# Products with v of even and odd heads in turn, in the two halves of TensorE's columns

## The chip, the cores and the metric

The kernel runs on one core of a Trainium2 chip. The metric is the time of one execution on the device in microseconds (us), the median of three runs.

The engines are TensorE (PE, matrix products and transposes), VectorE (DVE), ScalarE (ACT), GpSimd (POOL) and SyncE (SP, which issues most DMAs). Operands lie in SBUF, products land in banks of PSUM.

## The reference, cut to what matters

Two blocks are computed on 256 rows of 1024 channels in fp32: a feed-forward part, a mixer, a second feed-forward part, then an attention with forget gates ("fox") and a sparse attention ("dsa"). The change touches the mixer alone. It projects its input to q, k, v (8 heads of 64 channels) and u, runs an attention with a bias by relative position over q, k and v, a pooling over u, and projects both through `w_out`:

```python
def one_chunk(c):
    qb = lax.dynamic_index_in_dim(qc, c, axis=1, keepdims=False)
    kb = lax.dynamic_slice_in_dim(kp, c * CHUNK, BAND, axis=1)
    vb = lax.dynamic_slice_in_dim(vp, c * CHUNK, BAND, axis=1)
    s = jnp.einsum('bqhd,bkhd->bhqk', qb, kb).astype(jnp.float32) * scale + bias
    ...
    p = jax.nn.softmax(s, axis=-1)
    return jnp.einsum('bhqk,bkhd->bqhd', p.astype(vb.dtype), vb)

def hybrid_mixer(h, w_in, ..., w_out):
    ...
    a = chunked_attention(q, k, v, q_gain, k_gain, rel_bias)
    p = multiscale_pool(u, pool_w, pool_scale)
    return jnp.concatenate([a, p], axis=-1) @ w_out
```

## The kernel before

The 256 rows are two tiles, t = 0 and 1, of 128. Weights arrive as units of up to 128 x 1024 numbers (tile `raw`); ACT rounds each to fp32r (`whi`, L196), DVE takes the rest (`wlo`, L197), and a product with weights is three one-pass products into an `mm` bank (`half`, with `mm` at L163). `prefetch` keeps up to eight split units ahead. All products of the program are recorded at L163 and all transposes at L178; so the tiles' names tell them apart: `mm` with `op` is the projection of the pooling, `mm` with `oa` that of the attention, `sc` with `kT, qT` (or their parts) the scores, `tr` with `cst, s` the transposes of the softmax, `sc` with `pT, v` the products with v.

The order of the source around the change is made by a planner. `self.now` is a clock that each product and each transpose moves on by a fixed amount (0.109 us for a transpose). `later(us, fn)` puts a step on a heap with a due time, `when(keys, us, fn)` does so once events have fired, and `pump`, called behind every `half`, runs all steps that are due; `drain` runs all. The due times are in `DUE`: `mix_pv` 1.0, `mix_pv2` 4.74. The compiler then orders each engine's instructions by itself: they do not all run in the order of the source.

In the mixer, `scores(t, b)` multiplies q by k for a block of heads: t = 0 has one block of eight heads with 128 keys, t = 1 has two blocks of four heads with 256 keys. Even heads (e = 0) lie in channels 0 to 63 of each 128, odd heads (e = 1) in 64 to 127, and the two take turns, each in a `sc` bank of its own. Then, for each e, DVE adds the bias (L534), ACT and DVE compute the softmax (L443, L445, L538, L540), and `pv(t, b, e)` is planned. It transposes the probabilities in four products into a `tr` bank (`p_T`; there are two such banks) and copies them to a tile `pT` (L466; in turn by ACT and DVE; two buffers). Then `pv2(t, b, e)` runs four fp32 products with v, 64 columns of the array by 128 numbers, into partitions 64 e to 64 e + 63 of a `sc` bank `aT[t]`. Behind the last of a tile, `split_psum` (L238, L239) makes the fp32r pair `oa`, which the projection reads.

The output projection is issued around it: first the four halves on the pooling's result for t = 0, four for t = 1, then, behind a `drain`, the eight on the attention's. So there are projection products that do not need the attention while its steps wait for ACT and DVE.

Of the kernel before, what the change touches and what calls it, by code (L numbers as in the profile page):

```python
# [9 lines left out]
F32 = mybir.dt.float32  # L10
# [6 lines left out]
P = 128  # L17
# [28 lines left out]
def unit_list():  # L46
# [38 lines left out]
DUE = {  # L85
    "ffn_T": 6.0,
    "ffn_x": 3.0,
    "mix_T": 9.32,
    "mix_pool1": 1.21,
    "mix_pool2": 1.49,  # L90
    "mix_s": (0.5, 0.55, 3.0),
    "mix_pv": 1.0,
    "mix_pv2": 4.74,
# [20 lines left out]
class Kern:  # L114
# [330 lines left out]
            nc.scalar.activation(s[:, h, :], s[:, h, :], AF.Exp, bias=m[:, h:h + 1],  # L445
                                 accum_out=l[:, col + h:col + h + 1])

    def p_T(self, pool, s, nh, nk, split=False):

        ps = self.bank("tr")  # L450
        if split:
            n = nk // P
            v = ps.rearrange("p (k h q) -> p k h q", k=n, q=P)
            for k in range(n):
                for h in range(nh):
                    self.tr(v[:, k, h, :], s[:, h, k * P:(k + 1) * P])
            out = tuple(pool.tile([P, n, nh * P], F32R, name="pT" + c, bufs=2) for c in "hl")
            self.split_psum(*(o.rearrange("p k n -> p (k n)") for o in out), ps)
            return out
        v = ps.rearrange("p (h k q) -> p h k q", h=nh, q=P)  # L460
        for h in range(nh):
            for k in range(nk // P):
                self.tr(v[:, h, k, :], s[:, h, k * P:(k + 1) * P])
        out = pool.tile([P, 512], F32, name="pT", bufs=2)
        self.flip = not getattr(self, "flip", False)
        (self.nc.scalar.copy if self.flip else self.nc.vector.tensor_copy)(out, ps)  # L466
        return out.rearrange("p (h k q) -> p h k q", h=nh, q=P)


    def mixer(self, u, gain, next_gain):  # L470
        self.stage = "mix"
        nc, tc, A = self.nc, self.tc, self.A
        with tc.tile_pool(name="mix", bufs=1, reuse_waits="tile") as pool:
# [14 lines left out]
            v = [pool.tile([P, 512], F32, name=f"v{t}") for t in range(2)]  # L488
# [31 lines left out]
            def scores(t, b):  # L520

                nh, nk = (4, P) if t == 0 else (2, S)
                ps = [self.bank("sc").rearrange("p (h k) -> p h k", h=nh) for _ in range(2)]
                for i in range(nh):
                    for e in range(2):
                        j, r = nh * b + i, slice(64 * e, 64 * e + 64)
                        if t == 0:
                            self.mm(ps[e][:, i, :], qT[r, j, :], kT[r, j, :], True, True)
                        else:
                            self.mm3(ps[e][:, i, :], qTs, kTs, True, True, (r, j), (r, j))  # L530
                for e in range(2):
                    s = pool.tile([P, nh, nk], F32, name="s", bufs=6)
                    h0 = 2 * nh * b + e
                    nc.vector.tensor_tensor(s, ps[e], B[:, h0:h0 + 2 * nh - 1:2, S - nk:S], op=ALU.add)  # L534
                    l = self.small("ml", 4, bufs=4)
                    self.softmax_part(pool, s, nh, nk, l, 0)
                    ri = self.small("ri", 4, bufs=4)
                    nc.vector.reciprocal(ri[:, :nh], l[:, :nh])  # L538
                    for i in range(nh):
                        nc.vector.tensor_scalar(s[:, i, :], s[:, i, :], ri[:, i:i + 1], None, op0=ALU.mult)  # L540
                    self.when([("mix", "v")], DUE["mix_pv"], lambda e=e, s=s: pv(t, b, e, s, nh, nk))

            aT = {}

            def pv(t, b, e, s, nh, nk):
                pT = self.p_T(pool, s, nh, nk)
                self.later(DUE["mix_pv2"], lambda: pv2(t, b, e, pT, nh, nk))

            def pv2(t, b, e, pT, nh, nk):
                if b == e == 0:  # L550
                    aT[t] = self.bank("sc").rearrange("p (i q) -> p i q", i=4)
                for i in range(nh):
                    j = nh * b + i
                    for k in range(nk // P):
                        self.mm(aT[t][64 * e:64 * e + 64, j, :], v[k][:, 128 * j + 64 * e:128 * j + 64 * e + 64],
                                pT[:, i, k, :], k == 0, k == nk // P - 1)
                if e == 1 and nh * (b + 1) == 4:
                    self.split_psum(*oT[t, "a"], aT[t])

            dT = {}  # L560
# [28 lines left out]
            for t, acc in self.chunk(u, 4):  # L589
                qk_norm(acc, t, qT, qTs if t else None, _GAIN["q"], 0.125)  # L590
            u += 4
            self.when([("mix", "T", g, t) for g in (_GAIN["k"], _GAIN["q"]) for t in range(1)], DUE["mix_s"][0],
                      lambda: scores(0, 0))
            for b in range(2):
                self.when([("mix", "T", g, t) for g in (_GAIN["k"], _GAIN["q"]) for t in range(2)],
                          DUE["mix_s"][1 + b], lambda b=b: scores(1, b))
# [622 lines left out]
```

## Time and profile before

| | us |
|---|---|
| median of 3 runs | 729.85 (729.18 to 730.84) |
| the profiled execution | 731.11 |
| its span, from the first to the last instruction | 729.3 |
| PE busy in the span | 713.9 |
| DVE busy | 493.7 |
| ACT busy | 366.6 |

The profile shows one execution. PE is TensorE with its products, PEld its weight loads, which overlap with products. An fp32 product appears as two records, a transpose or an fp32r product as one. Products are pipelined and their ends are modelled, so starts are more exact than ends; merged rows give the start of the first and the time to the end of the last. The granted clock (PEclk) is a share of full speed.

### The profile page before, as it was taken

To read this page: it belongs to the slowest core of one execution; us is meant where nothing else is said; L and a number is where in the kernel's file an instruction comes from. 1 tells how busy PE (TensorE), PEld (TensorE's weight loads), DVE (VectorE), ACT (ScalarE), POOL (GpSimd) and SP (SyncE) were. 2 spreads that over 40 slices of the span, in tenths; PEclk is the share of its full clock that TensorE was granted. 3 is DMA by queue.
4 is the path that set the end of the run, shared out by engine and by line. 5 is a ranking of instruction groups with operands and counts; after the bars stand their busy time and mean duration, and the time that the engine had idled before them with its cause. 6 is when DMAs were issued, how large, how long until landed. Compare 5 with 4: busy or idle time off the path is not lost.

```text
span 729.3 us, 9860 instructions
## 1 busy us (share of the span) xinstructions
PE 713.9 (98%) x3608; PEld 597.6 (82%) x3608; DVE 493.7 (68%) x791; ACT 366.6 (50%) x544; POOL 58.2 (8%) x89
## 2 busy tenths in 40 slices
PE   8999999999999999999999999999999999999995
PEld 7788889888888778888889878878987889778984
DVE  6876766665647958665676556663555868998965
ACT  5654554354555736454454354554554625675820
POOL 0011110200003001101111200000000001000001
PEclk9999999999999999999999999999999999999998
DMA  7898656876735245667755767653560427533501
GB/s 261 296 320 294 228 205 217 272 266 195 264 103 204 85 149 171 209 202 252 264 200 198 275 217 229 237 158 111 193 232 29 143 66 253 208 116 116 173 1 58
DMA packets 42034, 139.80 MB, mean 192 GB/s; under 512 B 5362, under 2 KB 6530, under 8 KB 41858
## 3 DMA queue, kind: packets, MB, share of 16 engines
q1 hardware_dynamic: 37890, 127.23, 51.7%
q0 software_dynamic: 3808, 11.56, 4.6%
q8 instruction: 28, 0.46, 0.2%
q10 hardware_dynamic: 288, 0.39, 0.1%
q14 instruction: 20, 0.16, 0.1%
HBM read 132.34 MB, written 6.82 MB: 191 GB/s over the span
## 4 chain that ended last, share of the span: by engine, by line
PE 73%; DMA 11%; DVE 9%; issue 2%; ACT 2%; POOL 2%; SPq 0%; DVEq 0%; POOLq 0%; ACTq 0%
PE mm L163 63%; PE sc L163 6%; DVE wlo L197 4%; DMA raw<-in_w 3%; PE tr L178 3%; DMA hd<-d 3%; DMA d<-hb 2%; DMA rope<-in_rope 1%; POOL hrs L291 1%; ACT whi L196 1%; DMA row_final_norm<-in_final_norm 1%; PE tr L163 1%; POOL d L281 1%; DMA x<-in_x 1%; ACT s L445 0%
## 5 line engine op out<-in xcount | busy, mean ns | idle before, releaser
L197 DVE TENSOR_TENSOR wlo<-raw,whi 128x1024 fp32r<-128x1024 f32 (+3 forms) x236 | 273.9, 1175 | 86.4 <-ACT whi L196 82.8
L196 ACT CAST whi<-raw 128x1024 fp32r<-128x1024 f32 (+3 forms) x236 | 235.5, 1013 | 133.0 <-PE mm L163 82.5
L163 PE MATMUL mm<-whi,xl 128*128 128x512 f32 (+3 forms) x760 | 287.9, 380 | 1.6 <-DVE xl L325 0.8
L163 PE MATMUL mm<-wlo,xh 128*128 128x512 f32 (+3 forms) x760 | 284.1, 374 | 0.5 <-DVE wlo L197 0.2
L163 PE MATMUL mm<-whi,xh 128*128 128x512 f32 (+3 forms) x760 | 283.4, 374 | 0.0
L163 PEld LDWEIGHTS mm<-whi,xl 128*128 128x128 f32 x760 | 143.6, 189 | 25.8 <-DVE xl L325 1.0
L163 PEld LDWEIGHTS mm<-whi,xh 128*128 128x128 f32 x760 | 143.4, 189 | 24.0
L163 PEld LDWEIGHTS mm<-wlo,xh 128*128 128x128 f32 x760 | 143.7, 189 | 23.6 <-DVE wlo L197 1.8
L163 PE MATMUL mm<-whi,hl 128*128 128x512 f32 x176 | 68.7, 390 | 0.0
L163 PE MATMUL mm<-wlo,hh 128*128 128x512 f32 x176 | 68.5, 389 | 0.0
L163 PE MATMUL mm<-whi,hh 128*128 128x512 f32 x176 | 68.5, 389 | 0.0
L239 DVE TENSOR_TENSOR hl<-hd,hh 128x512 fp32r<-128x512 f32 (+1 forms) x24 | 14.5, 644 | 62.4 <-ACT hh L238 62.4
L238 ACT CAST hh<-hd 128x512 fp32r<-128x512 f32 (+1 forms) x24 | 12.8, 582 | 70.8 <-DMA hd<-d 70.8
L163 PEld LDWEIGHTS mm<-whi,hh 128*128 128x128 f32 x176 | 33.0, 188 | 6.9
L163 PEld LDWEIGHTS mm<-whi,hl 128*128 128x128 f32 x176 | 33.0, 188 | 6.8
L163 PEld LDWEIGHTS mm<-wlo,hh 128*128 128x128 f32 x176 | 33.1, 188 | 6.7
L281 POOL DMA_DIRECT2D d<-hb x48 | 26.4, 556 | 148.2 <-DVE hb L413 148.0
L400 ACT ACTIVATE th<-mm,hr 128x512 f32<-128x512 f32 (+1 forms) x24 | 15.6, 651 | 24.8 <-PE mm L163 24.8
L445 ACT ACTIVATE s<-s,nmax 128x128 f32<-128x128 f32 (+1 forms) x48 | 21.3, 446 | 12.8 <-DVE nmax L443 12.7
L291 POOL TENSOR_TENSOR rs<-ms,mhalf 128x1 f32<-128x1 f32 x10 | 6.5, 647 | 181.8 <-DVE ms L304 181.8
L402 DVE SCALAR_TENSOR_TENSOR a<-th,mm 128x512 f32<-128x512 f32 (+1 forms) x24 | 15.1, 630 | 5.2 <-ACT th L400 5.2
L411 DVE SCALAR_TENSOR_TENSOR h<-a,qr,mm 128x512 f32<-128x512 f32 (+1 forms) x24 | 16.7, 698 | 2.3 <-PE mm L163 2.3
(223 smaller groups left out, 598.6 us busy)
## 6 DMA issues: line engine op xcount, KB each, us to landing
raw<-in_w SPq DMA_DIRECT2D x208, 512.0 KB, 4.5
d<-hb POOLq DMA_DIRECT2D x40, 128.0 KB, 4.3
hd<-d POOLq DMA_DIRECT2D x10, 512.0 KB, 6.2
raw<-in_w SPq DMA_DIRECT2D x12, 344.0 KB, 3.2
raw<-in_w SPq DMA_DIRECT2D x8, 372.0 KB, 3.7
raw<-in_w SPq DMA_DIRECT2D x8, 256.0 KB, 4.6
x<-in_x SPq DMA_DIRECT2D x2, 512.0 KB, 4.6
B<-in_bias SPq DMA_DIRECT2D x1, 1024.0 KB, 5.6
```

The costliest lines, as they stand in the source:

```text
L163: self.nc.tensor.matmul(out, a, b, start=start, stop=stop)
L178: self.nc.tensor.transpose(out, a, self.ident[:p, :p])
L196: nc.scalar.copy(hi[:, :m], raw[:, :m])
L197: nc.vector.tensor_sub(lo[:, :m], raw[:, :m], hi[:, :m].bitcast(F32))
L238: nc.scalar.copy(hi, src)
L239: nc.vector.tensor_sub(lo, src, hi.bitcast(F32))
L281: self.nc.gpsimd.dma_start(out=d[a].rearrange("b i m -> i b m"), in_=src[32 * a:32 * a + 32])
L291: self.nc.gpsimd.tensor_tensor(out, a, self.mhalf[:, 0:1].to_broadcast(list(a.shape)), op=ALU.pow)
L400: nc.scalar.activation(th[:, :w], acc[:, :w], AF.Tanh, scale=hr[t])
L402: nc.vector.scalar_tensor_tensor(a[t][:, :w], th[:, :w], 1.0, acc[:, :w], op0=ALU.add, op1=ALU.mult)
L411: nc.vector.scalar_tensor_tensor(h[:, :w], a[t][:, :w], qr[t], acc[:, :w], op0=ALU.mult, op1=ALU.mult)
L445: nc.scalar.activation(s[:, h, :], s[:, h, :], AF.Exp, bias=m[:, h:h + 1], accum_out=l[:, col + h:col + h + 1])
```

## The change

`pv` and `pv2` of a block now handle both parities. `scores` collects the two tiles `s` in a list and plans one `pv` behind the loop instead of one per parity; `pv` transposes and copies both and plans one `pv2`, which issues eight products with e as the innermost loop, so that neighbours in the source write the two halves of the partitions of `aT[t]`. The tile `pT` of the mixer has four buffers instead of two. The number of products, transposes and copies is the same.

```diff
-    def p_T(self, pool, s, nh, nk, split=False):
+    def p_T(self, pool, s, nh, nk, split=False, bufs=2):
...
-        out = pool.tile([P, 512], F32, name="pT", bufs=2)
+        out = pool.tile([P, 512], F32, name="pT", bufs=bufs)
...
+                ss = []
                 for e in range(2):
                     s = pool.tile([P, nh, nk], F32, name="s", bufs=6)
+                    ss.append(s)
...
-                    self.when([("mix", "v")], DUE["mix_pv"], lambda e=e, s=s: pv(t, b, e, s, nh, nk))
+                self.when([("mix", "v")], DUE["mix_pv"], lambda: pv(t, b, ss, nh, nk))
 
             aT = {}
 
-            def pv(t, b, e, s, nh, nk):
-                pT = self.p_T(pool, s, nh, nk)
-                self.later(DUE["mix_pv2"], lambda: pv2(t, b, e, pT, nh, nk))
-
-            def pv2(t, b, e, pT, nh, nk):
-                if b == e == 0:
+            def pv(t, b, ss, nh, nk):
+                pT = [self.p_T(pool, s, nh, nk, bufs=4) for s in ss]
+                self.later(DUE["mix_pv2"], lambda: pv2(t, b, pT, nh, nk))
+
+            def pv2(t, b, pT, nh, nk):
+
+                if b == 0:
                     aT[t] = self.bank("sc").rearrange("p (i q) -> p i q", i=4)
                 for i in range(nh):
                     j = nh * b + i
                     for k in range(nk // P):
-                        self.mm(aT[t][64 * e:64 * e + 64, j, :], v[k][:, 128 * j + 64 * e:128 * j + 64 * e + 64],
-                                pT[:, i, k, :], k == 0, k == nk // P - 1)
-                if e == 1 and nh * (b + 1) == 4:
+                        for e in range(2):
+                            self.mm(aT[t][64 * e:64 * e + 64, j, :], v[k][:, 128 * j + 64 * e:128 * j + 64 * e + 64],
+                                    pT[e][:, i, k, :], k == 0, k == nk // P - 1)
+                if nh * (b + 1) == 4:
                     self.split_psum(*oT[t, "a"], aT[t])
```

## Rows read from the trace of the kernel before

**Rows 1.** The page's first part: busy us (share of the span) and instructions.

```profile
PE 713.9 (98%) x3608; PEld 597.6 (82%) x3608; DVE 493.7 (68%) x791; ACT 366.6 (50%) x544; POOL 58.2 (8%) x89
```

**Rows 2.** Chain of waits in order of time, 246 to 275: start, us, what.

```profile
247.30 1.58 PE sc L163 x11
...
262.64 10.90 PE mm L163 x47
```

**Rows 3.** Windows of 5 us: busy us (instructions) by engine, granted clock, DMA share, GB/s.

```profile
250.00:255.00 5.00, 5.00 (x31) 3.79 (x31) 5.00 (x14) 3.21 (x12) 0.00 (x0) 1.00 0.00 0
255.00:260.00 5.00, 5.00 (x31) 3.13 (x29) 1.85 (x5) 1.17 (x2) 0.00 (x0) 1.00 0.33 108
```

**Rows 4.** PE in order of time, products with v: start us, us, what, count.

```profile
251.89 0.40 PE L163 MATMUL mm<-whi,op 128*128 128x512 f32 x1
252.21 1.09 PE L163 MATMUL sc<-pT,v 128*64 128x128 f32 x8
253.23 0.50 PE L163 MATMUL mm<-whi,op 128*128 128x512 f32 x1
253.57 0.40 PE L163 MATMUL mm<-wlo,op 128*128 128x512 f32 x1
...
256.24 0.65 PE L163 MATMUL sc<-pT,v 128*64 128x128 f32 x4
256.82 0.66 PE L178 MATMUL tr<-cst,s 128*128 128x128 f32 x4
...
262.57 0.50 PE L163 MATMUL mm<-wlo,op 128*128 128x512 f32 x1
```

**Rows 5.** PE grouped by line and form, 252.3 to 262.5: busy us, mean ns, idle before.

```profile
L163 PE MATMUL sc<-pT,v 128*64 128x128 f32 x48 | 6.7, 282 | 0.0
L163 PE MATMUL mm<-whi,op 128*128 128x512 f32 x5 | 2.4, 478 | 0.0
L178 PE MATMUL tr<-cst,s 128*128 128x128 f32 x12 | 2.1, 286 | 0.0
L163 PE MATMUL mm<-wlo,op 128*128 128x512 f32 x2 | 0.8, 397 | 0.0
```

**Rows 6.** PE in order of time, the scores of tile 0, row halves in turn.

```profile
236.28 1.16 PE L163 MATMUL sc<-kT,qT 64*128 64x128 f32 x16
237.37 0.50 PE L163 MATMUL mm<-whi,xl 128*128 128x512 f32 x1
```

**Rows 7.** Weight loads and products, 260.05 to 260.2, where an odd block meets an even one.

```profile
260.10 0.20 PEld L163 LDWEIGHTS sc<-pT,v 128*64 128x64 f32 x4 [0.17 <-issue]
260.11 0.33 PE L163 MATMUL sc<-pT,v 128*64 128x128 f32 x2
```

**Rows 8.** PE in order of time, scores of tile 1: first block's ends, second block's ends.

```profile
245.14 0.39 PE L163 MATMUL sc<-kTsh,qTsl 64*128 64x256 f32 x2
...
245.84 0.29 PE L163 MATMUL sc<-kTsh,qTsh 64*128 64x256 f32 x2
...
247.30 0.38 PE L163 MATMUL sc<-kTsh,qTsl 64*128 64x256 f32 x1 [0.26 <-DVE s L534]
...
248.60 0.28 PE L163 MATMUL sc<-kTsh,qTsh 64*128 64x256 f32 x1
```

**Rows 9.** DVE in order of time: weight split, scalings, the copies that waited [idle before].

```profile
253.24 1.20 DVE L197 TENSOR_TENSOR wlo<-raw,whi 128x1024 fp32r<-128x1024 f32 x1
254.36 0.61 DVE L540 TENSOR_SCALAR s<-s,ri 128x256 f32<-128x256 f32 x2
...
255.69 0.69 DVE L466 COPY pT<-tr 128x512 f32<-128x512 f32 x1 [0.65 <-PE sc L163]
...
260.58 0.69 DVE L466 COPY pT<-tr 128x512 f32<-128x512 f32 x1 [3.07 <-PE sc L163]
```

**Rows 10.** Tile pT, 245 to 264, who waited for it: us, times.

```profile
PEld sc L163: 0.2, 1
```

**Rows 11.** PE in order of time, the first projection product on the attention.

```profile
267.92 0.39 PE L163 MATMUL mm<-whi,oa 128*128 128x512 f32 x1
```

**Rows 12.** PE's waits behind 252 us: us in total, times, longest (first of seven).

```profile
PE tr L178 <- DVE y L915: 1.0, 1, 1.0
```

## The prediction, made before the result was seen

> **What bounds the kernel now.** I read the page first. TensorE (PE) is busy for 98% of the span, its weight loads, which run under the products, for 82%, and the next engine, VectorE (DVE), for 68% [rows 1], so time that leaves PE's queue should leave the span unless something else is waiting right behind it. Next, the chain of waits over the mixer's attention. From 247.30 to 273.5 us it has only PE pieces, first scores, transposes and products with v, then the output projection as one piece of 47 products in 10.90 us [rows 2]. The windows agree: PE 5.00 busy in 5.00, granted clock 1.00, and DVE just as full up to 255 us, nearly idle behind it [rows 3]. So the stage that the change touches, 252.21 to 262.57 us, is paid for in PE time, and DVE is the runner-up in its first half.
>
> What fills these 10.36 us is in the grouping by form: 48 records of products with v, 12 transposes and 7 products of the output projection [rows 5]. An fp32 product leaves two records, so 48 are the 24 products of eight heads (eight for the first tile of rows, sixteen for the second). In the order of time they come in eight visits: 8, 8, 4, 4, 4, 2, 10 and 8 records, with transposes or projection products between (the fences show the first and the third) [rows 4].
>
> **What a record and a visit cost.** A visit of 8 records takes 252.21 to 253.23 = 1.02 us until the next product may start, one of 4 takes 256.24 to 256.82 = 0.58 [rows 4]: 0.11 a record and 0.14 fixed. Outside it, the first record follows the product before it by 0.32 (251.89 to 252.21) and the second product behind it stands 0.34 from the first (253.23 to 253.57), where the projection's products follow each other at 10.90 / 47 = 0.23 [rows 2, 4]: 0.20 more next to projection products, less next to transposes. As a sum: 46 records at 0.11 (two run beside two others, below) 5.06, 12 transposes at the same 0.11 (they stream the same 128 columns of fp32 in one record) 1.3, 7 products at 0.23 1.6, together 8.0. The stage takes 10.36, so eight visits hold 2.4 of overhead, **0.30 a visit**.
>
> **Part 1, halves in turn.** Now the four heads of one parity follow each other, all in one half of the columns: 0.11 a record, one after the other. Two rows bound what alternation gives. The scores of the first tile do the same with halves of the array's rows, also in fp32: 16 records from 236.28 to 237.37, 1.09 us, the time that 8 records with v take [rows 4, 6]. Less the fixed 0.14 that is 0.12 for a pair instead of 0.22. That is another axis of the array. But the trace of before has the columns once, by chance: at 260.11 the last product of odd heads meets the first of the next even block, two records start inside the same 0.33 us, and their four weight loads take 0.20 together [rows 7]. Column halves do run beside each other, both loads and products, in one PSUM bank. I take 0.12 a pair: 24 pairs 2.88 against 46 x 0.11 = 5.06, **2.2 gained**. The bounds are 0, if no pair forms, and 2.4 at 0.11 a pair.
>
> The Trainium skill speaks against this on TensorE: Matmul & The Clock Gate, Part 3 (The mechanism): weight loads overlap with running products only where the row groups differ. Two column halves share all rows, so by it the loads of the other half would wait and the 2.2 would go. Rows 7 show otherwise, in two pairs; I keep it as rival 2.
>
> **Part 2, blocks of both parities.** pv2 now runs once for eight products instead of twice for four, so three blocks take the place of six. Eight visits become three at best, and stay eight if transposes and projection products get between as now. The order of an engine in this trace is not the order of the source (transposes stand inside blocks that the source keeps whole, third visit in rows 4), so some splitting stays, and more of it can't be excluded. I take five: 3 x 0.30 = **0.9 gained**, bounds 0.6 lost (ten visits) and 1.5 gained.
>
> **Part 3, four pT buffers.** With two, DVE's second copy waits 0.65 for products that still read its buffer and its third 3.07 [rows 9]. With four, both parities of a block can be copied while the block before it is still multiplied, without which blocks of eight would have to wait for each other. The six copies themselves stay, three on DVE at 0.69 [rows 9] and three on ScalarE. Gain of its own: none, since PE had other products to do; if it were missing, part 1 would lose its second and third block.
>
> **Part 4, what moves.** The planner's clock counts 0.109 for a transpose, so pv2 of the first block is due 4 x 0.109 = 0.44 later. By the planner's own sums (a half of the projection 6 x 0.216 = 1.30, the six blocks' transposes 24 x 0.109 = 2.62) the third half ends at 6.51 behind v and pv2 was due at 1.30 + 0.44 + 4.74 = 6.47; it is now due at 6.91, so the blocks come behind the fourth half, six products. That costs PE nothing: these products have to run anyway, and the seven that stand inside the stage already [rows 5] are these six and one more. It would cost PE idle time if the attention's sum came too late for the projection on it, which starts at 267.92 [rows 11]. The sum for the second tile is complete at 262.57 [rows 4], 5.3 us before, with only products between that do not need it; these are still to come after the change, and the two split passes, about the size of a copy's 0.69 each, fit in. No DMA is issued in the moved steps, and no queue of SP or POOL is passed.
>
> **Part 5, a new wait.** A block needs both copies. The odd one is DVE's, and DVE is full until 255 us, with a 1.20 us weight split and two scalings of 0.61 together in the way [rows 3, 9]. Behind the waiting product, PE's queue stands still. Now PE waited there once, 0.2 us in all [rows 10]. A shorter stage brings PE to the same DVE results sooner: I take the same 0.2 once more, **0.2 lost**, bounds 0 and 1.8 a block (a split and two scalings) in rival 3.
>
> **Sum.** 2.2 + 0.9 - 0.2 = 2.9 us. The best case is 2.4 + 1.5 = 3.9. Behind the stage PE waits seven times, 3.9 us in all, the longest 1.0 [rows 12], each time for something computed from PE's own results, which moves with PE; no wait there is for a weight transfer. So I carry all 2.9 to the end. The profiled execution took 731.1 (span 729.3 and 1.8 around it) and would take 728.2. It stands 1.26 above the median of the runs; against that median of 729.85 the sum gives **727.0**.
>
> **Rivals.** 1. The pairs don't form. The second tile's scores show how: in the first block both halves run in pairs, 12 products in 245.14 to 245.84; in the next, written the same way, one half had to wait for DVE, all products of the other half went first, and the same 12 took 247.30 to 248.60 [rows 8]. If the even copy is ready before the odd one in each block, even products go first and odd ones follow, and the change doesn't do what it says. For it: DVE's backlog. Against it: four buffers let the copies run ahead, and eight products contiguous in the queue may still overlap as at 260.11. Left is a visit or two, 0.6: 729.2.
>
> 2. The other half's load waits for the running product (as by the Trainium skill's rule above). Then only the visits count: 3 to 5 visits, 0.9 to 1.5, here 1.2: 728.6. Rows 7 speak against it.
>
> 3. Slower: the wait for DVE's copy decides. Its place is the first odd product of each block, its price up to 1.8 us with PE's queue held, 5.4 for three blocks, and 5.4 - 2.9 = 2.5 slower: 732.4. It decides once these waits exceed 2.9. For it: DVE 5.00 of 5.00 until 255 [rows 3]. Against it: before, DVE spent 0.65 and 3.07 idle ahead of its last two odd copies [rows 9], waiting for buffers that are now free, so only the first two blocks can be late.
>
> 4. The gain is given back later: a shorter stage leaves less time for casts and splits of weights, and PE waits for them in the next feed-forward part. Against it: no such wait stands in the trace behind 252 us [rows 12]. The time would be that of before, 729.9.
>
> **How the numbers follow.** My forecast has 0.62, rival 1 0.14, rival 2 0.05, rival 3 0.09, rival 4 0.10. What the measurement can tell from no change is 0.2%, 1.46 us: faster below 728.4, slower above 731.3. Faster: the forecast, whose own range is 1.5 to 3.9 gained (726.0 to 728.4), and the best ends of rivals 1 and 2 (0.03), together 0.65. Slower: rival 3 and 0.01 of rival 4, 0.10. Same: what is left of rivals 1, 2 and 4, 0.25. The range runs from the best sum, 729.85 - 3.9 = 725.95 less 0.45 for the runs' own spread (they lie 0.7 below and 1.0 above their median), to rivals 1 and 4 with the same on top: 725.5 to 730.3. Rival 3 is left out.
>
> **What would show it.** In the trace after: records of products with v starting in pairs within a hundredth of a microsecond, 16 of them in about 1.1 us (step 1); three to five visits between 252 and 260 (step 2); copies of pT with no idle time put down to products (part 3); the first projection product on attention near 265 with no PE idle ahead of it (part 4); PE waits on pT or on transposes of 0.2 at most (part 5). PE's sum over the stage should fall by about 3. I am wrong if even and odd products still stand in separate runs, if a new wait on DVE appears in PE's list of waits, or if a later wait of PE has grown by what the stage lost.

## The result and the profile after

The changed kernel took **725.6 us** (median of four runs, 724.9 to 727.1), and the kernel before, run beside it on the same chip, 730.35. The ratio is 0.9943 with an interval of 0.9928 to 0.9958, so it is faster by 0.4 to 0.7%. The predicted 727.0 is 1.4 more. Two later comparisons of the same kernels gave 0.9951 and 0.9956. By these three ratios the change is worth 3.2 to 4.2 us, where the sum said 2.9. The first comparison is the outer one: its 725.6 lies 0.1 above the lower end of the stated range, and its 4.2 us exceed the best sum of 3.9. The two later ones, with twelve runs of the changed kernel each, give 3.6 and 3.2.

The profiled execution took 727.07, of which the span is 725.3. First the page of after, to be read beside [rows 1]: PE's busy time fell from 713.9 to 708.9, and nothing else moved by more than a few us.

```profile
PE 708.9 (98%) x3608; PEld 594.4 (82%) x3608; DVE 494.4 (68%) x791; ACT 368.2 (51%) x544; POOL 58.3 (8%) x89
```

A total of one execution against another holds more than the change. So I measure the stage between two marks that stand in every kernel: from the first product of the output projection behind the scores to the first one that uses the attention (`oa`, [rows 11] in before). The same instructions lie between them everywhere. Here are the windows between the marks, of before and then of after (busy us and instructions of PE, weight loads, DVE, ACT, POOL, then granted clock, DMA share, GB/s):

```profile
248.80:267.91 19.11, 19.11 (x107) 14.26 (x107) 13.08 (x27) 9.34 (x23) 0.00 (x0) 1.00 0.22 75
```

```profile
249.95:265.64 15.69, 15.69 (x107) 12.26 (x107) 13.00 (x27) 9.26 (x23) 0.00 (x0) 1.00 0.27 87
```

The same 107 PE instructions, PE never idle, at granted clock 1.00 (the 2.4 GHz level) in both; but **19.1 us became 15.7, 3.44 gained** (by the starts of the marks, 19.12 and 15.68). This gain does not depend on the execution: the stretch was 19.13 in a second one of before, and 15.68 in both further ones of the changed kernel.

Next, the visits in PE's order of time (start, us, what, count), which answer to [rows 4]:

```profile
255.20 1.31 PE L163 MATMUL sc<-pT,v 128*64 128x128 f32 x18
256.44 0.66 PE L178 MATMUL tr<-cst,s 128*128 128x128 f32 x4
257.40 0.40 PE L163 MATMUL mm<-whi,op 128*128 128x512 f32 x1
257.73 0.44 PE L163 MATMUL sc<-pT,v 128*64 128x128 f32 x4
258.10 0.66 PE L178 MATMUL tr<-cst,s 128*128 128x128 f32 x4
258.69 0.88 PE L163 MATMUL sc<-pT,v 128*64 128x128 f32 x12
259.49 0.50 PE L163 MATMUL mm<-whi,op 128*128 128x512 f32 x1
259.92 1.09 PE L163 MATMUL sc<-pT,v 128*64 128x128 f32 x14
260.94 0.50 PE L163 MATMUL mm<-wlo,op 128*128 128x512 f32 x1
...
265.65 0.39 PE L163 MATMUL mm<-whi,oa 128*128 128x512 f32 x1
```

Read the last visit: 14 records from 259.92 until the next product at 260.94, 1.02 us, the time that eight took before [rows 4]. Its first two records start in the same 0.33 us, and their four weight loads take 0.20 together, as in [rows 7]:

```profile
259.92 0.20 PEld L163 LDWEIGHTS sc<-pT,v 128*64 128x64 f32 x4 [0.24 <-issue]
259.92 0.33 PE L163 MATMUL sc<-pT,v 128*64 128x128 f32 x2
```

There are 22 pairs in the stage that start within 0.01 of each other, where before had two. (A record does not name its half; that the two of a pair are an even and an odd one is read from the source.) There are four visits (18, 4, 12, 14) instead of eight, and the first one holds the first block of eight heads whole and two records of the next.

Last, DVE in order of time, the copies, beside [rows 9]:

```profile
253.73 0.68 DVE L466 COPY pT<-tr 128x512 f32<-128x512 f32 x1
254.40 1.20 DVE L197 TENSOR_TENSOR wlo<-raw,whi 128x1024 fp32r<-128x1024 f32 x1
...
256.12 0.67 DVE L466 COPY pT<-tr 128x512 f32<-128x512 f32 x1
...
258.79 0.69 DVE L466 COPY pT<-tr 128x512 f32<-128x512 f32 x1 [0.88 <-PE tr L178]
```

No copy waits for products any more (0.65 and 3.07 before); the last waits 0.88 for its own transposes, which is only order. PE nowhere waits for pT.

### The profile page after: what moved, and what is told of

Read it like the earlier page. It is cut to its first block, busy times and chain, and to the rows that moved or that the text cites. A ratio compares the mean times of both kernels' runs of the same rounds, so it can differ in the third digit from the quotient of the medians.

```text
span 725.3 us, 9858 instructions
## 1 busy us (share of the span) xinstructions
PE 708.9 (98%) x3608; PEld 594.4 (82%) x3608; DVE 494.4 (68%) x791; ACT 368.2 (51%) x544; POOL 58.3 (8%) x89
## 4 chain that ended last, share of the span: by engine, by line
PE 84%; DVE 6%; DMA 4%; ACT 2%; issue 1%; POOL 1%; SPq 0%; DVEq 0%; ACTq 0%; POOLq 0%
PE mm L163 75%; PE sc L163 6%; PE tr L178 3%; DMA raw<-in_w 2%; DVE wlo L197 2%; POOL hrs L291 1%; DMA row_final_norm<-in_final_norm 1%; PE tr L163 1%; DMA x<-in_x 1%; ACT whi L196 1%; ACT s L445 0%; ACT sq L302 0%; DVE hss L497 0%; DVE kn L505 0%; DVE xl L245 0%
## 5 line engine op out<-in xcount | busy, mean ns | idle before, releaser
L239 DVE TENSOR_TENSOR hl<-hd,hh 128x512 fp32r<-128x512 f32 (+1 forms) x24 | 14.4, 644 | 43.2 <-ACT hh L238 43.2
L238 ACT CAST hh<-hd 128x512 fp32r<-128x512 f32 (+1 forms) x24 | 12.8, 583 | 51.0 <-DMA hd<-d 51.0
L400 ACT ACTIVATE th<-mm,hr 128x512 f32<-128x512 f32 (+1 forms) x24 | 15.7, 652 | 30.6 <-PE mm L163 30.4
L445 ACT ACTIVATE s<-s,nmax 128x128 f32<-128x128 f32 (+1 forms) x48 | 21.3, 446 | 12.8 <-DVE nmax L443 12.8
```

Source lines behind the costliest of these rows:

```text
L238: nc.scalar.copy(hi, src)
L239: nc.vector.tensor_sub(lo, src, hi.bitcast(F32))
L400: nc.scalar.activation(th[:, :w], acc[:, :w], AF.Tanh, scale=hr[t])
```

## The experiments

The theory: the gain is PE time in this stage, from pairs and from fewer visits. The rivals: the visits alone do it (no gain from the order inside a block), or the buffers alone, or the later place of the blocks behind the fourth half. The stretch between the marks is the measure throughout; it repeats to 0.03 us between executions of one kernel. Here it is for all kernels. A pair is two records that start within 0.02 us of each other. Where whole runs of the two halves follow each other, records also run beside each other half a record apart (0.05 to 0.06); the column does not count these.

| kernel | stretch, us | records per visit | pairs |
|---|---|---|---|
| before (twice) | 19.12, 19.13 | 8, 8, 4, 4, 4, 2, 10, 8 | 2 |
| buffers only | 18.13 | 8, 16, 4, 2, 10, 8 | 3 |
| merged blocks, halves not in turn | 17.11 | 18, 10, 2, 10, 8 | 5 |
| changed, two buffers | 16.80 | 2, 14, 6, 10, 2, 14 | 18 |
| changed, due earlier | 16.09 | 2, 16, 4, 12, 14 | 22 |
| **changed** (three times) | 15.68 | 18, 4, 12, 14 | 22 |
| changed, due later (twice) | 14.72, 14.69 | 48 | 22 |
| due later, in turn by two products | 14.70 | 48 | 11 |
| due later, in turn by four products | 15.23 | 48 | 5 |
| due later, longest runs | 16.01 | 48 | 3 |

**The changed kernel again.** Nothing is edited. The first ran beside the merged blocks, the buffers only and the later due time, the second beside the earlier due time, the longest runs and the repeat of the later due time.

> The changed kernel once more, as a measure for the others on the same chip. By the trace of its first profile, PE's start times fall behind those of before by 3.5 us over the stage of products with v, by 1.1 more at the start of the fox attention (where before had waited 0.9 for a DVE addition), and are 1.2 late from the first 26 us on. If the first and last of these three belong to single executions and not to the change, this run shows the 3.5 again and not the other two, and the time stands 3.5 us (0.5%) below before; if the change causes the 1.1 as well, 4.6 us (0.6%).

> The changed kernel a third time, beside the one above: 15.7 us for the stretch, and 3.5 to 4.2 us below before.

Measured: 725.83 us, 0.9951 (0.9936 to 0.9966), and 726.2 us, 0.9956 (0.9941 to 0.9971). Their stretches are 15.68 like the first one's. What differs between their totals lies elsewhere (below, behind the experiments).

**Merged blocks without turns.** Four buffers and blocks of both halves, as changed, but all even products of a block first:

```diff
-                for i in range(nh):
-                    j = nh * b + i
-                    for k in range(nk // P):
-                        for e in range(2):
+                for e in range(2):
+                    for i in range(nh):
+                        j = nh * b + i
+                        for k in range(nk // P):
```

> As the changed kernel, but inside a block the four (or the remaining) products of even heads come first and those of odd heads behind them; blocks, buffers and due times stay. Theory: the two column halves work through their own products as soon as these stand in PE's queue, as the scores of tile 1 did with runs of three (pairs within 0.01 us), so runs of four in one visit pair as well: the stage gains about 3.5 us and the time equals the changed kernel's. Rival: products must alternate one by one; then a visit of eight products takes about 0.11 x 16 + 0.15 = 1.9 us instead of 1.1, and only the saved visits are left: about 0.9 us in the stage, 729.

Measured: 727.61 us, 0.9972 (0.9956 to 0.9988); stretch 17.11. So 2.0 of the 3.44 come without any turn-taking, and the turns add 1.43. Both expectations miss: runs of four do not pair as a whole, and they gain more than the saved visits alone. PE in order of time:

```profile
253.17 1.58 PE L163 MATMUL sc<-pT,v 128*64 128x128 f32 x18
254.68 0.66 PE L178 MATMUL tr<-cst,s 128*128 128x128 f32 x4
...
258.67 1.09 PE L163 MATMUL sc<-pT,v 128*64 128x128 f32 x8
259.69 0.50 PE L163 MATMUL mm<-wlo,op 128*128 128x512 f32 x1
```

The last visit has one half only: eight records in 1.02, as before. The first has 18 records of both halves, one run behind the other, and takes 1.51 to the transposes, 0.5 less than 18 at 0.11 alone. In the record starts, the first odd one (253.660) stands beside the fifth of the eight even ones (253.655), not behind the last: where two runs touch, they overlap by some records.

**Buffers only.** The kernel before, with four pT buffers and its own blocks and order:

```diff
-                pT = self.p_T(pool, s, nh, nk)
+                pT = self.p_T(pool, s, nh, nk, bufs=4)
```

> The kernel before with four buffers for pT and nothing else: even and odd blocks stay apart. Theory that pairing gives most of it: pairs form only where an odd run happens to follow an even one in the same visit; 0.6 to 1.7 us gained over the stage, 728 to 729.5. Rival: the copies' waits for buffers (0.65 and 3.07 us on DVE before) were what cost the time, and the alternation is decoration: about 3.5 us gained, 726.

Measured: 729.08 us, 0.9994 (0.9975 to 1.0013), which the total can't tell from no change; but the stretch is 18.13, 1.0 less than before. That is inside the expected 0.6 to 1.7, and the rival's 3.5 falls. Two visits went, and in one place an even and an odd run touch, 16 records in 1.51 instead of twice 8 in 1.02:

```profile
253.58 1.58 PE L163 MATMUL sc<-pT,v 128*64 128x128 f32 x16
255.09 0.50 PE L163 MATMUL mm<-whi,op 128*128 128x512 f32 x1
```

**The change with two buffers.**

```diff
-                pT = [self.p_T(pool, s, nh, nk, bufs=4) for s in ss]
+                pT = [self.p_T(pool, s, nh, nk, bufs=2) for s in ss]
```

> The changed kernel with two buffers for pT instead of four. Theory: a block's copies wait until the block before has read its buffers, so the products come in more visits (six instead of four) but still in pairs: the stretch from the first projection product to the first on the attention's result takes 15.7 + 2 x 0.32 = 16.3 us. Rival of the prediction (without the buffers, the second and third block lose their pairs): up to 1.5 more, 17.8.

Measured: 730.0 us (one run); stretch 16.80, 0.5 above the 16.3 expected and 1.0 below the rival. Six visits instead of four and 18 pairs instead of 22: 2 x 0.32 + 4 x 0.11 = 1.1, which is the difference to 15.68. The stage still gains 2.3. That the total nevertheless equals that of the second execution of before (729.79) has causes elsewhere: its first mark already stood 1.4 later (249.11 against 247.74), PE's wait for y, 207 us behind the stage, was 1.0 longer (2.38 against 1.38, the longest of that wait in all executions), and the clock fell behind it, which costs 1.2 (last section); its later waits were shorter and gave 1.0 of this back.

**The place of the blocks.** The due time of pv2, earlier by the 0.44 that the merged blocks' transposes add, and later:

```diff
-    "mix_pv2": 4.74,
+    "mix_pv2": 4.3,
```

```diff
-    "mix_pv2": 4.74,
+    "mix_pv2": 7.2,
```

> The changed kernel with pv2 due 4.3 instead of 4.74 behind its transposes, so that it is issued behind the third half of the projection as before the change. Prediction: the move behind the fourth half cost nothing, so the stretch takes 15.7 us again, or 0.3 more for each visit more. Rival: the later issue is what let both copies be ready and the pairs form; then pairs are lost and the stretch takes 16.5 or more.

> The changed kernel with the products with v due 7.2 instead of 4.74 behind their transposes, so that in the order of PE's instructions all 24 stand in one visit in place of four. Theory (a visit costs 0.30 us beside its products): 3 x 0.30 = 0.9 us below the changed kernel. Rival: the attention's sum is now late for the projection on it and PE waits there; each us that it comes later than the last projection product that doesn't need it shows as PE idle time ahead of the first product on oa, and the time is that of the changed kernel or above.

> The kernel with one visit a second time, beside the changed one: 14.7 us for the stretch against 15.7, so about 1.0 us (0.13%) below the changed kernel and 4.6 to 5 below before, if nothing behind it gives it back; equal to the changed kernel, if PE's later waits take it up.

Measured: earlier, 725.32 us (one run) and a stretch of 16.09, 0.41 more than the changed kernel's with one visit more. Later, 724.92 us, 0.9934 (0.9913 to 0.9956), and a second time 726.7, 0.9948 (0.9926 to 0.997); stretches 14.72 and 14.69. PE in order of time when later, with all three blocks in one visit:

```profile
257.54 3.00 PE L163 MATMUL sc<-pT,v 128*64 128x128 f32 x48
260.47 0.50 PE L163 MATMUL mm<-whi,op 128*128 128x512 f32 x1
...
263.32 0.39 PE L163 MATMUL mm<-whi,oa 128*128 128x512 f32 x1
```

From four visits to one with the same 22 pairs is 15.68 - 14.71 = 0.97, so a visit costs 0.97 / 3 = **0.32** on average; the one visit that the earlier due time adds costs 0.41. The later due time makes the stage 1.0 shorter in both executions, and the projection on the attention still follows 2.9 behind the last product with v, without a wait. In the total its intervals overlap those of the changed kernel, so a version better than the changed one is shown for the stage and not for the whole.

**How long a run may be.** On top of the later due time, which puts all 48 records in one visit, I let the halves alternate by runs of two products (four records; the diff), by four (the same with 4 for 2), and in the longest runs that the blocks hold (the second diff):

```diff
+                ik = [(i, k) for i in range(nh) for k in range(nk // P)]
+                for r in range(0, len(ik), 2):
+                    for e in range(2):
+                        for i, k in ik[r:r + 2]:
...
```

```diff
-                    for k in range(nk // P):
-                        for e in range(2):
-                            self.mm(aT[t][64 * e:64 * e + 64, j, :], v[k][:, 128 * j + 64 * e:128 * j + 64 * e + 64],
+                    for e in range(2):
+                        for k in range(nk // P):
+                            h, c = (b, 2 * i + e) if t else (i // 2, 2 * (i % 2) + e)
+                            self.mm(aT[t][64 * h:64 * h + 64, c, :], v[k][:, 128 * j + 64 * e:128 * j + 64 * e + 64],
...
```

> The kernel with all 24 products in one visit (14.72 us over the same stretch, 2.93 from its first record to the next product), now with two even products, then two odd, and so on. Theory from the runs of four (there the first odd record started beside the fifth of eight even ones): PE starts work of the other half about four records ahead, so runs of two products, four records, still pair fully: 2.93 and 14.7 again. Rival: only neighbours pair, so that one product in two runs alone: 12 of 24 pairs are lost, 12 x 0.11 = 1.3 more.

> The same with four even products, then four odd ones, in each of the three blocks. Theory of a reach of about four records: at each of the five changes of the half, four records run beside four others, so of 48 records 20 are hidden; (48 - 20) x 0.11 + 0.2 = 3.3 us from the first record to the next product instead of 2.93, and 15.1 for the stretch. Rival, no reach limit: 2.93 and 14.7. Rival, only neighbours pair: 5 products hidden, (48 - 10) x 0.11 + 0.2 = 4.4, and 16.2.

> The kernel with all products with v in one visit, with the halves of the columns given out by head and block instead of by parity: four products in the first half, four in the other, then eight and eight. It puts the attention's results in other places of the sum, so its output isn't the reference's; number and size of products, transposes and copies are the same. Theory (only the alternation of the halves gives time, with a reach of about four records): 12 of 48 records run beside others, 36 x 0.11 + 0.3 = 4.3 us for the visit instead of 2.93, and 16.1 for the stretch from the first projection product to the first one on the attention's result instead of 14.7. Rival (the gain is from one visit and blocks of eight, not from the halves): 2.9 and 14.7.

Measured (one run each: 724.84, 724.67 and 728.18 us): the visit of 48 records takes 2.93 in turn by single products and 2.95 in turn by two, 3.49 by four (3.3 was expected), and 4.24 in the longest runs (8, 8, 16 and 16 records; 4.3 was expected). First the end marks of runs of two, then of four, then the longest:

```profile
256.90 3.02 PE L163 MATMUL sc<-pT,v 128*64 128x128 f32 x48
259.85 0.50 PE L163 MATMUL mm<-whi,op 128*128 128x512 f32 x1
```

```profile
257.08 3.56 PE L163 MATMUL sc<-pT,v 128*64 128x128 f32 x48
260.57 0.50 PE L163 MATMUL mm<-whi,op 128*128 128x512 f32 x1
```

```profile
257.64 4.32 PE L163 MATMUL sc<-pT,v 128*64 128x128 f32 x48
261.88 0.50 PE L163 MATMUL mm<-whi,op 128*128 128x512 f32 x1
```

How far the second half runs ahead can be counted. These are the records begun in the first 0.54 us of the visit in turn by two products, and those begun in the first 0.48 and 0.54 of the one by four:

```profile
256.90 0.82 PE L163 MATMUL sc<-pT,v 128*64 128x128 f32 x10
```

```profile
257.08 0.65 PE L163 MATMUL sc<-pT,v 128*64 128x128 f32 x4
```

```profile
257.08 0.82 PE L163 MATMUL sc<-pT,v 128*64 128x128 f32 x6
```

In runs of four products (eight records) four even records run alone, and the fifth starts together with the first odd one (257.569 and 257.575). So the other half's work begins while four records of the running half are still to come. The longest runs show the same four at each of their contacts. (That the record at 257.575 is the first odd one is read from the order of the source; the trace does not show the order in which the compiler queued a block's products, and no run here separates its part from the array's.) Counted as slots of 0.109 plus the 0.14 that a visit holds in itself: at four records of overlap for each contact of the halves, five contacts leave 28 slots, 3.19 (measured 3.49), three contacts leave 36, 4.06 (4.24), and no overlap would be 48, 5.37. That accounts for most of it. The rest is about 0.05 a contact: the half that comes in has its second record 0.16 behind its first, not 0.109, as every visit has at its start.

**The kernel before again.**

> The kernel before, for a second trace. The stretch from the first projection product behind the scores to the first one on the attention's result took 19.12 us in its first trace. If the 1.1 us that the changed kernel's trace gains near 436 us (PE waited 0.9 there for a DVE addition, before) comes from the single execution, that wait is smaller or gone here; if the change takes it away, it is here again with 0.9.

Measured: 729.79 us, stretch 19.13. The wait of 0.9 near 436 us is gone in it, so the change does not take it away; the other waits far from the stage are read in the next section.

## Why the prediction was right

The direction and the mechanism held. The stage gained 3.44 against a sum of 2.9, because two terms were mis-sized in the same direction: the visits by 0.4 and the wait on DVE by 0.2. That the first median nearly left the range at its fast end is not the stage's doing ("The total", below).

**Part 1, pairs.** Right. 22 pairs and four single records make 26 slots where before had 46: 20 x 0.109 = 2.18, against 2.2 predicted. The two errors in it cancel: pairs cost 0.109 and not the 0.12 borrowed from the scores [rows 6], and two of the 24 do not form. Column halves behave as rows 7 had it. Not all of it needed turns: the five visits of the merged blocks without turns take 4.77 in all, which less 0.14 each is 37 slots, so runs that only touch gave about 9 of the 20, the turns the other 11. Rivals 1 and 2 fall with this: even and odd products do not stand apart, and the loads of the other half do not wait. The Trainium skill, on TensorE: Matmul & The Clock Gate, Part 3 (The mechanism), lets weight loads overlap with running products only where the row groups differ; here all rows are shared and only the columns differ, and 14 records pass in 1.02 us where they would need 1.5 one behind the other. The measurement decides.

**Part 2, visits.** Right in kind, undersized. The eight became four, not five, at 0.32 and not 0.30: 4 x 0.32 = 1.28 against 0.9. The later due time shows that one was to be had. Together, 2.18 + 1.28 = 3.46, where the stretch lost 3.44; that is closer than the spread of a visit's price, 0.32 to 0.41, lets one expect.

**Part 3, buffers.** "Gain of its own: none" was wrong. Alone, in the kernel before, the two extra buffers take 1.0 from the stretch. The step that failed was "since PE had other products to do": PE did not idle for a buffer, but the other products that it did in the meantime cut the products with v into visits, at 0.32 each, and kept an odd and an even block from touching. The second half of the sentence was right in its mechanism: with two buffers the changed kernel has four pairs fewer, but it loses as much by two more visits, 1.1 in all. So of the 3.44, added in this order, about 1.0 comes by the buffers, 1.0 by merging the blocks (18.13 to 17.11), and 1.4 by the turns (17.11 to 15.68).

**Part 4, the move.** Right that it costs nothing, with a sign missed: putting the blocks back to their old place makes a visit more, 0.41 (0.3 expected). Moving them still further gains 1.0. The cover that I named, 5.3 us between the sum and the projection on it, is what allows it: now 260.94 to 265.65, 4.7, and 2.9 with the later due time, both without a wait.

**Part 5, the wait on DVE.** Mis-sized: 0.2 was taken and none came. With two buffers more DVE's copies wait for no products: at 253.73 and 256.12 they follow straight on its other work, and all three end 0.4 to 0.9 before the visit that needs them starts. Rival 3 falls with it. ("Nearly idle" behind 255 us was too strong a reading, DVE is busy 1.85 of 5.00 there [rows 3]; nothing in the sum rests on it.)

**What lies behind the stage** held in its result, but the step "each time for something computed from PE's own results ... no wait there is for a weight transfer" was wrong. The list of waits names the last link only. Followed back, at least three of the seven end with a transfer: the wait for x near 437 us (0.9) with one of weights, the first of the two for DVE's y (0.4, at 618.80) with one of `rope`, and that for ACT's y (0.8) with the row of norm weights. Pieces of the chain of before that ended last, in order of time:

```profile
428.32 5.31 DMA raw<-in_w
...
464.37 5.98 DMA row_final_norm<-in_final_norm
...
608.90 8.78 DMA rope<-in_rope
```

I followed the third through all executions. PE in the final part waits for ACT's y, ACT for DVE's x, and DVE (L735 of the changed kernel, L731 of before) for the row of norm weights. DVE in order of time, then PE, after:

```profile
466.92 1.28 DVE L735 SCALAR_TENSOR_TENSOR x<-x,rs,row_final_norm 128x1024 f32<-128x1024 f32 x1 [1.25 <-DMA row_final_norm<-in_final_norm]
```

```profile
471.24 0.44 PE L178 MATMUL tr<-cst,y 128*128 128x128 f32 x2 [0.96 <-ACT y L715]
```

The same two in the second execution of the later due time:

```profile
465.18 1.28 DVE L735 SCALAR_TENSOR_TENSOR x<-x,rs,row_final_norm 128x1024 f32<-128x1024 f32 x1 [2.47 <-DMA row_final_norm<-in_final_norm]
```

```profile
469.50 0.44 PE L178 MATMUL tr<-cst,y 128*128 128x128 f32 x2 [2.17 <-ACT y L715]
```

In all fourteen profiled executions PE's wait is DVE's wait for this transfer less 0.30, from 1.07 and 0.77 (in one of before and one of the changed kernel alike) to 2.67 and 2.38 with two buffers; where DVE waited only 0.39, PE waited 0.10. It differs as much between executions of one kernel as between kernels, and is as short with the shorter stage as without it. The reason is that the transfer moves along with PE: in all fourteen it is issued 9.55 us before PE runs out of other work. What varies is its own time from issue to landing, 5.3 to 7.6 us, and PE waits for what it takes beyond 5.2 (5.98 and 0.77 in before, 7.38 and 2.17 in the execution just shown). So a wait for a transfer can take up part of a gain, as rival 4 had it, but a shorter stage does not bring it about: these executions show no return of the gain. Why the transfer's time varies stays open.

**The total.** The two profiled executions differ by 4.0, the stretch by 3.44. Of the remaining 0.6, some goes both ways: PE's starts are 1.16 later in after already behind the first 26 us (its first waits, for xl and for the split weights, are 2.1 and 1.3 there), and about 1.1 of the gain comes at 437 us, from a wait of before behind a late weight transfer that the second execution of before does not have either. Neither belongs to the change. I carried the sum from a single execution of before as if its waits belonged to the kernel; they differ by about 1 us each from one execution to the next, which is as much as the smaller terms of the sum. So what the comparisons give beyond the stage's 3.44, or short of it, is no part of the change that any run here shows.

## What to carry to other kernels

Small fp32 products that use half of the array's columns (here 128 rows by 64 columns, 128 columns streamed) run two at a time if the other half's products stand within a few instructions behind them: let the halves take turns in runs of no more than two products, and give both halves' operands buffers enough to be ready together. Count how often an engine's queue changes from one kind of product to another, since each change has a price of its own, and buffers and due times set that number even where the engine never idles. A wait's releaser in a list of waits is only the last link: follow it back engine by engine to see whether a transfer stands at its end.

## What the runs showed of the hardware

**Reach of the array's queue.** TensorE began products of the other column half while four records of the running half were still to come, by the order of the source, so runs of two products (four records) lose next to nothing (2.95 against 2.93) and runs of four lose 0.56.

**Price of a change of kind.** 0.32 us on average over three visits of half-column products between full-width ones (0.41 for another one), with 0.14 of it inside the visit.

**The clock behind a wait.** In four of the fourteen executions the granted clock fell to the lower level, 1.2 GHz, behind the wait for y: with waits of 1.82, 2.17 and 2.38, and with one of 1.51 (the longest runs). In the ten others, with waits of 0.10 to 1.69, it stayed at the upper, 2.4 GHz. As it fell behind 1.51 and stayed behind 1.68 and 1.69, the length of this wait alone does not decide. Windows of 470 to 475 of the second execution with the later due time, then of the first (columns as above):

```profile
470.00:475.00 5.00, 4.95 (x16) 3.91 (x17) 2.31 (x3) 1.30 (x2) 0.00 (x0) 0.66 0.36 125
```

```profile
470.00:475.00 5.00, 5.00 (x24) 4.01 (x25) 3.10 (x4) 3.08 (x4) 0.00 (x0) 1.00 0.39 117
```

The same for the longest runs, behind the wait of 1.51:

```profile
470.00:475.00 5.00, 4.01 (x12) 3.09 (x13) 2.70 (x4) 1.86 (x3) 0.81 (x1) 0.72 0.58 193
```

And the products of the second execution behind its wait of 2.17:

```profile
471.22 0.63 PE L163 MATMUL mm<-whi,xl 128*128 128x512 f32 x1
471.65 0.63 PE L163 MATMUL mm<-wlo,xh 128*128 128x512 f32 x1
472.07 0.63 PE L163 MATMUL mm<-whi,xh 128*128 128x512 f32 x1
```

They come every 0.43, where at the upper level they come every 0.23 [rows 2]; in five microseconds that is 16 instructions instead of 24. From the first transpose behind the wait to the 60th PE record after it, 14.0 to 14.4 us pass where the clock fell and 12.8 where it stayed, so the lower clock costs 1.2 to 1.6. It happened to the changed kernel once in three profiled executions, to its later version once in two, and to the ones with two buffers and with the longest runs in their only ones, and it is a part of why their totals differ by more than their stages. The executions differ in what PE did ahead of the wait, too, and no run here separates the two.
